# Half-width products, masks and updates in a blocked triangular inversion, with the factor's identity columns written by GpSimd

## The chip, the core and the metric

The kernel runs on one core of one Trainium2 chip. The core has five engines that work in parallel, each through its own list of instructions in order: PE (TensorE, matrix products; its weight loads are listed apart as PEld and overlap the products), DVE (VectorE), ACT (ScalarE), POOL (GpSimd) and SP, which here only issues DMAs. The metric is the device time of the run in microseconds (us); lower is better. Times of single instructions and of waits come from one execution recorded by the hardware profiler.

## What is computed

The reference is one inference step of a two-layer decoder: layer 0 mixes tokens with a gated delta rule in chunks, layer 1 with a short gated convolution; each layer also attends to 256 memory tokens, and there are 2048 prompt tokens and 64 sample tokens. The part that the change touches is the triangular solve of the delta rule in layer 0:

```
A = jnp.tril(jnp.einsum('bnhid,bnhjd->bnhij', kb, k) * decay, -1)
wu = lax.linalg.triangular_solve(A + jnp.eye(C, dtype=A.dtype), rhs, left_side=True,
                                 lower=True, unit_diagonal=True)
```

The kernel builds the inverse of I + A for 128 tokens at a time (for the 64 sample tokens in blocks of 8) and applies it as a product.

## The kernel before

**Stages.** Layer 0 takes six heads over four prompt tiles of 512 tokens and one sample tile of 64. For each head and tile it projects keys, queries, values and a gate out of 1024 inputs (`proj`: 24 products of 128x512 into one PSUM bank, named `psp` in the rows), convolves and activates them on ACT and DVE, builds the matrix and its inverse (the `wy_` jobs), scans the four chunks one after the other with the head's state (`scan`, bank `psA`) and writes the gated output. Then come the attention, the output projection, and layer 1, which has no inversion.

**Order.** Nothing is scheduled on the chip. The kernel writes its program through `Flow`, a planner: every step is a Python generator (a job), and whenever the planner's own PE clock is free, it runs the job of the highest priority that is ready by then. Ready times come from a table of costs: `mm` charges a product 3 + columns / 2.4 ns (at least 64 columns), `Eng` charges the other engines by elements, `HOPS` the way from engine to engine. Buffers are handed out by credits (`Credit`, `Sub`): a job that wants a buffer yields until one has been put back. Since each engine works in program order, an instruction whose input is late holds up everything behind it on its engine. A changed cost therefore moves instructions of unrelated jobs.

**The inversion** is `wy_inv`. One job holds a pair of chunks (`hc` = 2, both of 128 tokens; the sample tile has one of 64). It is started twice for each prompt tile, 48 times in all, with 6 levels each (`lv` = 7), and 6 times for the sample tiles, with 2 levels: 48 x 6 + 6 x 2 = 300 levels. The tile `ul` holds the inverse so far, as U (transposed) and L, each with two 128x128 matrices in 16-bit floats. `A16` (`A` in the rows, since numbers are cut from names; the listings of order print `A_1568` and the like) holds the scaled matrix. At level `li` the blocks of size 2^li on the diagonal are already inverted, and pairs of them are joined:

- PE: `pq` = A16 times L, 2 products of 128 columns. Release: the ACT copy of the level before.
- DVE: `qq` = `pq` times a mask `masks[:, li]`, 256 elements per partition, out of PSUM. The mask keeps the block below the diagonal and the diagonal itself, so that `qq` is an identity plus the blocks.
- PE: `pu`, 4 products of 128 columns: `qq` with U, and U with `qq`.
- ACT: copies `pu` back over U and L, 512 elements per partition in one instruction.

After the last level come a correction (`pe`, `ee`) and the last product into `u`. POOL works beside this: it adds the scaled identity (`M`), makes the first U, the low part `Ml` of the matrix, the tables `gm` of the decays, the low halves of the projection weights (`whl`) and of the normed input (`ht`), and small powers (`rk`, `rq`, `hr`).

The buffers `qq`, `A16`, `Ml`, `ee` and `gm` come from one ring of 12 (`NKQ`, credit `kqc`); before the change a `qq` was taken only after `pq`, and put back right behind the `pu` products.

Of the kernel before, what the change touches and what calls it, by code (L numbers as in the profile page):

```python
# [15 lines left out]
AF = mybir.ActivationFunctionType  # L16
ALU = mybir.AluOpType
# [269 lines left out]
def hybrid_kernel(  # L287
# [18 lines left out]
    fl = Flow()  # L306
# [43 lines left out]
    def wait(*flags):  # L350
        for f in flags:
            if not f.on or f.t + HOP > fl.cur.t:
                yield f
# [20 lines left out]
    kqc = Credit(fl, NKQ)  # L374
# [3 lines left out]
    def const(shape, dt, name):  # L378
        return cp.tile(shape, dt, tag=name, name=name)
# [7 lines left out]
    def psum(tag, shape, bufs, name):  # L387
        t = pp.tile(shape, F32, tag=tag, name=name, bufs=bufs)
        psum_names.add(t.tensor.name)
        return t  # L390
# [4 lines left out]
    def gbank(name):  # L395
        return psum("bank", [P, 4, P], 8, name)
# [10 lines left out]
    def k1(name, dt=F32):  # L407
        return gp.tile([P, 2, P], dt, tag="k1", name=name, bufs=NK1)
# [4 lines left out]
    def kq16(name):  # L413
        return gp.tile([P, 2, P], F16, tag="kq", name=name, bufs=NKQ)
# [439 lines left out]
    identh = const([P, P], F16, "identh")  # L854
# [5 lines left out]
    masks = const([P, 7, P], F16, "masks")  # L860
# [539 lines left out]
    def rows(x, n, C):  # L1400
        return x[:n, :n].rearrange("p (o f) -> p o f", o=1).to_broadcast([n, C, n])
# [150 lines left out]
    def wy_inv(it, i):  # L1552

        n, hc = it.n, it.hc
        lv = 7 if n == P else 3
        yield from wait(it.M_ok[i])
        M = it.M[i]  # L1560
        G.tensor_tensor(M[:n, :hc, :n], M[:n, :hc, :n], rows(identKh, n, hc), op=ALU.add)
        yield
        yield from ulc.get()
        yield from kqc.get(2)
        A16 = kq16("A16")
        V.tensor_copy(A16[:n, :hc, :n], M[:n, :hc, :n])
        UL = gp.tile([P, 4, P], F16, tag="k1", name="ul", bufs=NK1)
        U, L = UL[:n, 0:2], UL[:n, 2:4]
        yield
        yield from gc_.get()  # L1570
        pq = gbank("pq")
        for z in range(hc):
            mm(pq[:n, z, :n], A16[:n, z, :n], identh[:n, :n])
        t = fl.cur.t
        G.tensor_tensor(U[:, :hc, :n], A16[:n, :hc, :n], rows(mask_u, n, hc), op=ALU.mult)
        fl.cur.t, fl.cur.eng = t, "PE"
        yield
        V.tensor_tensor(L[:, :hc, :n], pq[:n, :hc, :n], rows(masks[:, 0], n, hc), op=ALU.mult)
        gc_.put()
        yield  # L1580
        Ml = None
        for li in range(1, lv):
            yield from gc_.get()
            pq = gbank("pq")
            for z in range(hc):
                mm(pq[:n, z, :n], A16[:n, z, :n], L[:, z, :n])
            if Ml is None:
                t = fl.cur.t
                Ml = kq16("Ml")
                G.tensor_tensor(Ml[:n, :hc, :n], M[:n, :hc, :n], A16[:n, :hc, :n], op=ALU.subtract)  # L1590
                fl.cur.t, fl.cur.eng = t, "PE"
                Mc.put()
            yield
            yield from kqc.get()
            qq = kq16("qq")
            V.tensor_tensor(qq[:n, :hc, :n], pq[:n, :hc, :n], rows(masks[:, li], n, hc), op=ALU.mult)
            gc_.put()
            yield
            yield from gc_.get()
            pu = gbank("pu")  # L1600
            for z in range(hc):
                mm(pu[:n, z, :n], qq[:n, z, :n], U[:, z, :n])
            for z in range(hc):
                mm(pu[:n, 2 + z, :n], U[:, z, :n], qq[:n, z, :n])
            kqc.put()
            yield
            if hc == 2:
                A.activation(UL[:n, :, :n], pu[:n, :, :n], AF.Copy)
            else:
                A.activation(UL[:n, 0:4:2, :n], pu[:n, 0:4:2, :n], AF.Copy)  # L1610
            gc_.put()
            yield
        yield from gc_.get()
        pe = gbank("pe")
        for z in range(hc):
            mm(pe[:n, z, :n], A16[:n, z, :n], L[:, z, :n], start=True, stop=False)
            mm(pe[:n, z, :n], Ml[:n, z, :n], L[:, z, :n], start=False, stop=True)
        yield
        kqc.put(2)
        yield from kqc.get()  # L1620
        ee = kq16("ee")
        V.tensor_tensor(ee[:n, :hc, :n], rows(identKh, n, hc), pe[:n, :hc, :n], op=ALU.subtract)
        gc_.put()
        yield
        yield from uc.get()
        yield from gc_.get()
        pu = gbank("pu1")
        for z in range(hc):
            mm(pu[:n, z, :n], ee[:n, z, :n], U[:, z, :n])
        kqc.put()  # L1630
        yield
        it.u[i] = k1("u1")
        V.scalar_tensor_tensor(it.u[i][:n, :hc, :n], pu[:n, :hc, :n], 1.0 / MS, U[:, :hc, :n], op0=ALU.mult, op1=ALU.add)
        gc_.put()
        ulc.put()
        fl.set(it.u_ok[i])
# [170 lines left out]
    def head_tile(hd, t):  # L1807
# [13 lines left out]
        for i, (blk, w, dst) in enumerate(((6 + h, wk, kt_), (h, wq, qt_), (12 + h, wv, v_))):  # L1821
# [23 lines left out]
            if i == 0:  # L1845
                fl.spawn(3, chain(start, wy_decay(it)), "decay")
                fl.spawn(3, chain(start, wy_k(it, dn[0])), "wy_k")
                for z in range(it.nh):
                    fl.spawn(1, wy_inv(it, z), f"inv{z}")
            elif i == 1:  # L1850
                fl.spawn(3, chain(start, wy_q(it, dn[1])), "wy_q")
            else:
                fl.spawn(3, chain(start, wy_v(it, dn[2])), "wy_v")
# [449 lines left out]
```

## Time and profile before

| | |
|---|---|
| time, median of 3 runs | 2224.36 us (2221.85 to 2230.78) |
| time of the profiled execution | 2225.13 us |
| its span, first to last instruction | 2223.4 us |
| PE busy | 2147.2 us, 97% |
| DVE, ACT, POOL busy | 1488.9, 1120.7, 714.3 us |
| instructions of PE, DVE, ACT, POOL | 16176, 4228, 2952, 901 |
| levels of the inversion, and the stretch they lie in | 300, from 128 to 1050 us |

A row of busy time gives the union of an engine's instructions. PE's products are pipelined: one lasts some 0.2 to 0.4 us in the record, but the next one starts much sooner, so the distance between starts is what a product costs when PE has enough to do.

### The profile page before, as it was taken

The numbers are of one execution on the slowest core, as the hardware profiler recorded it, in microseconds if no ns is written. First come the engines' busy times: TensorE is split into PE (matmuls) and PEld (weight loads), VectorE is DVE, ScalarE is ACT, GpSimd is POOL, SyncE is SP. The second block draws the span as 40 slices with busy tenths as digits, with TensorE's granted clock in tenths as the row PEclk, the third lists the DMA queues.
The fourth block names the chain that finished last, engine by engine and source line by source line (L and its number), as shares of the span: only waits on it lengthen the run. The fifth ranks groups of instructions, "written<-read, shape, count | busy, mean of one in ns | idle before, by whom it ended". The sixth has DMA issues, their size and how long they took to land.

```text
span 2223.4 us, 43011 instructions
## 1 busy us (share of the span) xinstructions
PE 2147.2 (97%) x16176; PEld 1298.0 (58%) x16176; DVE 1488.9 (67%) x4228; ACT 1120.7 (50%) x2952; POOL 714.3 (32%) x901
## 2 busy tenths in 40 slices
PE   6889989999999999999999999999999999999998
PEld 5467657667666666666555454455444456555457
DVE  6988887887889878777777566355342437675354
ACT  5757665566657656566566345134221226653221
POOL 5655334442434433433222335012110212201322
PEclk9989999999999999999999999999999999999999
DMA  4201020201122102002134443022010111223433
GB/s 134 64 13 37 16 49 9 55 30 27 39 70 41 50 6 46 31 6 69 56 102 143 142 152 114 15 68 80 31 54 10 53 49 58 69 72 129 129 112 118
DMA packets 113634, 141.50 MB, mean 64 GB/s; under 512 B 50193, under 2 KB 67857, under 8 KB 113425
## 3 DMA queue, kind: packets, MB, share of 16 engines
q1 hardware_dynamic: 113424, 138.75, 20.5%
q8 instruction: 127, 2.08, 0.4%
q14 instruction: 83, 0.67, 0.1%
HBM read 99.22 MB, written 39.49 MB: 62 GB/s over the span
## 4 chain that ended last, share of the span: by engine, by line
PE 58%; DVE 3%; ACT 1%; issue 1%; DMA 1%; POOL 0%; POOLq 0%; DVEq 0%; ACTq 0%
PE psp L330 49%; PE psA L330 2%; PE psc L334 1%; PE pu L330 1%; PE po L330 1%; PE psc L330 1%; PE rb L330 1%; DVE wmx L281 1%; PE pq L330 1%; PE pqk L330 0%; DVE amx L281 0%; PE pkk L330 0%; DMA wraw<-in_wo 0%; DVE apT L281 0%; PE po L334 0%
## 5 line engine op out<-in xcount | busy, mean ns | idle before, releaser
L330 PE MATMUL psp<-ht,whl 128*128 128x512 f16 x5376 | 1270.0, 380 | 0.0
L330 PEld LDWEIGHTS <-whl 128*128 128x128 f16 x9408 | 753.6, 98 | 650.1 <-issue 12.6
L281 POOL TENSOR_TENSOR whl<-wraw,whl 128x512 f16<-128x512 f32 x184 | 216.8, 1182 | 448.0 <-ACT whl L281 400.2
L330 PE MATMUL psp<-hl,whl 128*128 128x512 f16 (+1 forms) x1728 | 342.4, 357 | 0.0
L281 ACT ACTIVATE ul<-pu 128x512 f16<-128x512 f32 x300 | 168.3, 582 | 79.6 <-PE pu L330 76.8
L281 ACT ACTIVATE wraw<-wraw,wsc 128x512 f32<-128x512 f32 (+1 forms) x186 | 131.7, 712 | 76.3 <-DVE wsc L281 44.6
L281 DVE SCALAR_TENSOR_TENSOR cacc<-psp,cws,cacc 128x511 f32<-128x511 f32 (+2 forms) x216 | 159.4, 738 | 10.1 <-ACT cacc L281 9.8
L281 POOL TENSOR_TENSOR nsq<-nsq 128x512 f32<-128x512 f32 (+2 forms) x105 | 100.6, 960 | 194.3 <-ACT nsq L281 149.1
L281 DVE TENSOR_TENSOR qq<-pq,masks 128x256 f16<-128x256 f32 x300 | 118.0, 407 | 51.1 <-PE pq L330 49.2
L281 DVE TENSOR_REDUCE wmx<-wraw 128x1 f32<-128x1024 f32 (+1 forms) x93 | 111.5, 1201 | 31.6 <-DMA wraw<-in_wb 24.5
L281 ACT ACTIVATE wg<-psp,hisc 128x512 f32<-128x512 f32 x64 | 44.0, 687 | 171.6 <-PE psp L330 171.4
L281 ACT ACTIVATE nsq<-xo 128x512 f32<-128x512 f32 (+1 forms) x72 | 41.4, 580 | 150.8 <-DVE xo L281 86.8
L281 ACT ACTIVATE whl<-wraw 128x512 f16<-128x512 f32 x184 | 114.8, 626 | 2.7
L281 DVE SCALAR_TENSOR_TENSOR xo<-psp,isc,xo 128x512 f32<-128x512 f32 (+1 forms) x72 | 49.6, 688 | 95.2 <-PE psp L330 95.2
L281 DVE SCALAR_TENSOR_TENSOR wg<-wg,psp 128x512 f32<-128x512 f32 x64 | 43.6, 681 | 87.8 <-ACT wg L281 87.8
L330 PEld LDWEIGHTS <-A 128*128 128x128 f16 x792 | 69.4, 100 | 41.1 <-issue 10.4
L281 ACT ACTIVATE ape<-psc,amx,sa 128x256 f32<-128x256 f32 x128 | 70.8, 561 | 31.7 <-DVE amx L281 31.6
L330 PE MATMUL pu<-ul,qq 128*128 128x128 f16 (+1 forms) x588 | 81.8, 224 | 3.9 <-DVE qq L281 3.1
L330 PE MATMUL pq<-ul,A 128*128 128x128 f16 (+1 forms) x588 | 77.0, 224 | 4.6 <-ACT ul L281 2.6
L330 PE MATMUL pu<-qq,ul 128*128 128x128 f16 (+1 forms) x588 | 81.2, 223 | 0.0
L281 POOL TENSOR_TENSOR rk<-sse,mhalf 128x4 f32<-128x4 f32 (+1 forms) x30 | 27.6, 919 | 159.9 <-DVE sse L281 118.8
L281 DVE SCALAR_TENSOR_TENSOR raw<-psp,wisc,cg 128x512 f32<-128x512 f32 x24 | 18.0, 749 | 86.9 <-PE psp L330 86.8
(344 smaller groups left out, 3641.0 us busy)
## 6 DMA issues: line engine op xcount, KB each, us to landing
br_sp<-wg SPq DMA_DIRECT2D x64, 256.0 KB, 2.0
brl<-br_sp SPq DMA_DIRECT2D x64, 256.0 KB, 2.9
wraw<-in_wb SPq DMA_DIRECT2D x28, 512.0 KB, 3.5
wraw<-in_wa SPq DMA_DIRECT2D x24, 512.0 KB, 3.5
xk<-in_x SPq DMA_DIRECT2D x64, 128.0 KB, 2.9
wraw<-in_wo SPq DMA_DIRECT2D x16, 512.0 KB, 3.4
xo<-in_x SPq DMA_DIRECT2D x32, 256.0 KB, 3.5
x_sp<-xo SPq DMA_DIRECT2D x32, 256.0 KB, 2.4
```

Source lines behind the costliest of these rows:

```text
L281: return f(out, *args, **kw)
L330: nc.tensor.matmul(out, lhsT=lhsT, rhs=rhs, start=start, stop=stop)
L334: nc.tensor.transpose(out, in_, ident)
```

## The change

At a level, only half the columns change: of L, in each pair of blocks the first block's columns; of U, the second's. The other columns of the products repeat what is there already, and the second blocks' columns of `qq` are plain identity columns. The change uses this in all 300 levels:

- `pq` and `pu` are made for 64 columns instead of 128 (32 instead of 64 in the sample tiles). The moving operand is read in runs of 2^li elements with gaps as long; the result lies packed in PSUM. The stationary operands keep their size.
- The DVE mask works on half the elements, with the mask and the output read and written in those runs.
- The ACT copy becomes two, one for U and one for L, of 128 elements each, written in runs.
- The identity columns of `qq` are now written by POOL (`unit`, 300 new instructions: identity times identity into the other half). The first is placed ahead of the levels, each further one right behind the `pu` products of the level before. Its buffer is thus taken a level ahead, directly after the former `qq` was put back.

```
-                mm(pq[:n, z, :n], A16[:n, z, :n], L[:, z, :n])
+                mm(pq[:n, z, :nb], A16[:n, z, :n], first[0][:, z])
...
-            V.tensor_tensor(qq[:n, :hc, :n], pq[:n, :hc, :n], rows(masks[:, li], n, hc), op=ALU.mult)
+            mask = halves(masks[:n, li:li + 1], li)[0].to_broadcast([n, hc, nb, 1 << li])
+            V.tensor_tensor(qf[:, :hc], pq[:n, :hc, :nb], mask, op=ALU.mult)
...
-                mm(pu[:n, z, :n], qq[:n, z, :n], U[:, z, :n])
+                mm(pu[:n, z, :nb], qq[:n, z, :n], second[1][:, z])
...
-                mm(pu[:n, 2 + z, :n], U[:, z, :n], qq[:n, z, :n])
+                mm(pu[:n, 2 + z, :nb], U[:, z, :n], qf[:, z])
+            t = fl.cur.t
             kqc.put()
+            if li + 1 < lv:
+                yield from kqc.get()
+                qq = unit(li + 1)
+            fl.cur.t, fl.cur.eng = t, "PE"
...
-                A.activation(UL[:n, :, :n], pu[:n, :, :n], AF.Copy)
+            A.activation(second[1][:, :hc], pu[:n, :hc, :nb], AF.Copy)
+            A.activation(first[0][:, :hc], pu[:n, 2:2 + hc, :nb], AF.Copy)
```

The new functions are

```
+        def halves(x, li):
+            v = x[:, :, :n].rearrange("p z (b h s) -> p z b h s", h=2, s=1 << li)
+            return v[:, :, :, 0], v[:, :, :, 1]
+        def unit(li):
+            qq = kq16("qq")
+            i2 = halves(idh, li)[1].to_broadcast([n, hc, n >> (li + 1), 1 << li])
+            G.tensor_tensor(halves(qq[:n], li)[1][:, :hc], i2, i2, op=ALU.mult)
+            return qq
```

Since the planner's costs of these steps change, all engines' lists are rearranged from the first inversion on. On PE the first `pu` products of the program stood like this (names: `ht` is the normed input, `whl` a projection's weights; in brackets the engines whose semaphores the instruction waits for):

```order
L330 MATMUL psp<-ht,whl 128x512
L330 LDWEIGHTS qq [waits PE_49,DVE_49]
L330 MATMUL pu<-ul,qq 128x128 [waits Pool_49]
L330 LDWEIGHTS qq
L330 MATMUL pu<-ul,qq 128x128
L330 LDWEIGHTS ul
L330 MATMUL pu<-qq,ul 128x128
```

and in the changed kernel the first ones read

```order
L330 MATMUL psp<-ht,whl 128x512
L330 LDWEIGHTS qq [waits DVE_49,Pool_49]
L330 MATMUL pu<-ul,qq 128x64 [waits PE_49]
L330 LDWEIGHTS qq
L330 MATMUL pu<-ul,qq 128x64
L330 LDWEIGHTS ul
L330 MATMUL pu<-qq,ul 128x64
```

The products have half the columns, as many weight loads stand before them, and the load of `qq` now waits for POOL as well as for DVE.

On POOL, the difference around the first two inversions is this (`A_1568` and `A_1606` are their matrices; `+` is new, the bare rows stand in both):

```order
 L281 TENSOR_TENSOR ul<-A_1606,mask_u 128x256
 L281 TENSOR_TENSOR ht<-nhs,ht 128x256
+L281 TENSOR_TENSOR qq<-identh 128x64x2
 L281 TENSOR_TENSOR Ml<-M,A_1568 128x256
 L281 TENSOR_TENSOR gm<-sLh,ghl 128x256 x2
+L281 TENSOR_TENSOR qq<-identh 128x64x2
+L281 TENSOR_TENSOR Ml<-M,A_1606 128x256
+L281 TENSOR_TENSOR ht<-nhs,ht 128x256 x3
+L281 TENSOR_TENSOR qq<-identh 128x32x4 x2
+L281 TENSOR_TENSOR rk<-sse,mhalf 128x4
+L281 TENSOR_TENSOR gm<-sLh,ghl 128x256 x2
+L281 TENSOR_TENSOR qq<-identh 128x16x8 x2
```

The identity columns of a level (`128x64x2`: 64 runs of 2, for both chunks) stand between the work for the next tiles, sometimes behind a power (`rk`) that waits for DVE.

On ACT, at the same place:

```order
-L281 ACTIVATE kd<-pk,eGlG 128x128 x4
-L281 ACTIVATE kt<-cacc 128x512
-L281 ACTIVATE cacc<-psp,cws 128x512
-L281 ACTIVATE ul<-pu 128x512 x2
+L281 ACTIVATE kt<-cacc 128x512
+L281 ACTIVATE cacc<-psp,cws 128x512
+L281 ACTIVATE kd<-pk,eGlG 128x128 x4
+L281 ACTIVATE ul<-pu 128x64x2 x4
+L281 ACTIVATE dd<-pd 128x256
 L281 ACTIVATE ht<-nhs 128x256
 L281 ACTIVATE qt<-cacc 128x512
```

Two copies of 512 elements have become four of 128 (64 runs of 2), and the neighbouring steps of the key's chain have changed places.

## Rows read from the trace of the kernel before

**Rows 1.** The page: busy time and share of each engine; granted PE clock, tenths, 40 slices.

```profile
PE 2147.2 (97%) x16176; PEld 1298.0 (58%) x16176; DVE 1488.9 (67%) x4228; ACT 1120.7 (50%) x2952; POOL 714.3 (32%) x901
...
PEclk9989999999999999999999999999999999999999
```

**Rows 2.** The page: the chain that ended last, shares by engine.

```profile
PE 58%; DVE 3%; ACT 1%; issue 1%; DMA 1%; POOL 0%; POOLq 0%; DVEq 0%; ACTq 0%
```

**Rows 3.** Stretches: us, busy PE, PEld, DVE, ACT, POOL (instructions), PE clock, DMA share, GB/s.

```profile
0.00:125.00 125.00, 97.01 (x616) 62.98 (x617) 96.74 (x279) 76.49 (x206) 74.00 (x111) 0.97 0.28 88
125.00:1055.00 930.00, 902.49 (x7488) 620.19 (x7487) 758.08 (x2443) 587.57 (x1792) 370.59 (x512) 0.99 0.14 35
1055.00:2223.40 1168.40, 1147.68 (x8076) 614.82 (x8075) 634.05 (x1508) 456.60 (x954) 269.74 (x279) 0.99 0.26 84
```

**Rows 4.** Who PE waited for from 125 to 1055 us: total, times, longest.

```profile
PE psA L330 <- ACT vh L281: 4.3, 1, 4.3
PE pu L330 <- DVE qq L281: 3.1, 6, 1.2
PE pq L330 <- ACT ul L281: 2.6, 5, 1.6
```

**Rows 5.** Groups of the inversion's steps, 125 to 1055 us: busy, mean ns | idle before.

```profile
L330 PE MATMUL pq<-ul,A 128*128 128x128 f16 x576 | 74.5, 224 | 4.6 <-ACT ul L281 2.6 <-DVE ssq L281 1.2 <-issue 0.4
L330 PE MATMUL pu<-ul,qq 128*128 128x128 f16 x576 | 79.2, 224 | 3.9 <-DVE qq L281 3.1
L281 DVE TENSOR_TENSOR qq<-pq,masks 128x256 f16<-128x256 f32 x288 | 115.7, 415 | 48.1 <-PE pq L330 46.4 <-PE psp L330 0.4
L281 ACT ACTIVATE ul<-pu 128x512 f16<-128x512 f32 x288 | 165.6, 595 | 76.5 <-PE pu L330 73.7 <-PE psp L330 1.6
```

**Rows 6.** PE in order of time: start, us, instruction, count; products of 128 and 64 columns.

```profile
536.79 0.28 PE L330 MATMUL pu<-ul,qq 128*128 128x128 f16 x2
...
537.12 0.28 PE L330 MATMUL pu<-qq,ul 128*128 128x128 f16 x2
537.23 0.81 PE L330 MATMUL psp<-ht,whl 128*128 128x512 f16 x3
...
539.23 0.60 PE L330 MATMUL psp<-hs_t,whl 128*128 128x64 f16 x15
539.66 0.47 PE L330 MATMUL psA<-vh,kd 128*128 128x128 f32 x2
```

**Rows 7.** Groups nearest to the new steps, 125 to 1055 us.

```profile
L281 DVE TENSOR_TENSOR o<-qs,psA 128x128 f32<-128x128 f32 x89 | 24.7, 278 | 0.0
L281 ACT ACTIVATE jk<-pqt 128x128 f32<-128x128 f32 x88 | 24.5, 278 | 9.1 <-PE pqt L334 6.9
L281 POOL TENSOR_TENSOR hm<-nhs,hm 128x128 f16<-128x128 f32 x8 | 3.4, 430 | 8.2 <-ACT hm L281 7.1 <-DVE qq L281 1.2
L281 POOL TENSOR_TENSOR gm<-sLh,ghl 64x64 f16<-64x64 f16 x12 | 3.2, 290 | 0.0
L281 POOL TENSOR_TENSOR ul<-A,mask_u 128x256 f16<-128x256 f16 x46 | 31.1, 686 | 21.7 <-DVE A L281 20.4 <-POOL dd L281 0.8 <-PE pq L330 0.2
L281 POOL TENSOR_TENSOR rk<-sse,mhalf 128x4 f32<-128x4 f32 x23 | 23.3, 1011 | 126.9 <-DVE sse L281 99.6 <-DVE halo L281 12.8 <-ACT kd L281 8.1
```

**Rows 8.** ACT in order of time: four copies with a pointer scale; two of 512 elements.

```profile
523.09 1.17 ACT L281 ACTIVATE kd<-pk,eGlG 128x128 f32<-128x128 f32 x4
...
537.27 1.08 ACT L281 ACTIVATE ul<-pu 128x512 f16<-128x512 f32 x2 [0.59 <-PE pu L330]
```

**Rows 9.** POOL and DVE at 200 us; one DVE step: group; durations min/median/max.

```profile
200.00 2.09 POOL L281 TENSOR_TENSOR ht<-nhs,ht 128x256 f16<-128x256 f32 x3 [4.53 <-ACT ht L281]
...
200.88 0.59 DVE L281 SCALAR_TENSOR_TENSOR cacc<-halo,cws,cacc 128x1 f32<-128x1 f32 x1
...
L281 DVE SCALAR_TENSOR_TENSOR cacc<-halo,cws,cacc 128x3 f32<-128x3 f32 x160 | 48.9, 305 | 0.0
...
L281 DVE SCALAR_TENSOR_TENSOR cacc<-halo,cws,cacc x162: 198/209/3218, 119.5 to 1009.9; 128x1 f32<-128x1 f32 x54, 128x2 f32<-128x2 f32 x54, 128x3 f32<-128x3 f32 x54
```

More of the change, by code (lines that the diff above doesn't have):

```diff
@@ L1581, in wy_inv @@
         Ml = None
+        def halves(x, li):
+            v = x[:, :, :n].rearrange("p z (b h s) -> p z b h s", h=2, s=1 << li)
+            return v[:, :, :, 0], v[:, :, :, 1]
+        idh = identh[:n, :n].rearrange("p (o f) -> p o f", o=1)
+        def unit(li):
[4 more added lines that the diff above has]
+        yield from kqc.get()
+        qq = unit(1)
+        fl.cur.t, fl.cur.eng = t, "PE"
         for li in range(1, lv):
+            nb = n >> (li + 1)
+            first, second = halves(L, li), halves(U, li)
+            qf = halves(qq[:n], li)[0]
             yield from gc_.get()
-            pq = gbank("pq")
+            pq = gbank("pq").rearrange("p c (b s) -> p c b s", s=1 << li)
             for z in range(hc):
-                mm(pq[:n, z, :n], A16[:n, z, :n], L[:, z, :n])
+                mm(pq[:n, z, :nb], A16[:n, z, :n], first[0][:, z])
+            t = fl.cur.t
             if Ml is None:
-                t = fl.cur.t
                 Ml = kq16("Ml")
                 G.tensor_tensor(Ml[:n, :hc, :n], M[:n, :hc, :n], A16[:n, :hc, :n], op=ALU.subtract)
-                fl.cur.t, fl.cur.eng = t, "PE"
                 Mc.put()
+            fl.cur.t, fl.cur.eng = t, "PE"
             yield
-            yield from kqc.get()
-            qq = kq16("qq")
-            V.tensor_tensor(qq[:n, :hc, :n], pq[:n, :hc, :n], rows(masks[:, li], n, hc), op=ALU.mult)
+            mask = halves(masks[:n, li:li + 1], li)[0].to_broadcast([n, hc, nb, 1 << li])
+            V.tensor_tensor(qf[:, :hc], pq[:n, :hc, :nb], mask, op=ALU.mult)
             gc_.put()
@@ L1599, in wy_inv @@
             yield from gc_.get()
-            pu = gbank("pu")
+            pu = gbank("pu").rearrange("p c (b s) -> p c b s", s=1 << li)
             for z in range(hc):
-                mm(pu[:n, z, :n], qq[:n, z, :n], U[:, z, :n])
+                mm(pu[:n, z, :nb], qq[:n, z, :n], second[1][:, z])
             for z in range(hc):
-                mm(pu[:n, 2 + z, :n], U[:, z, :n], qq[:n, z, :n])
+                mm(pu[:n, 2 + z, :nb], U[:, z, :n], qf[:, z])
+            t = fl.cur.t
             kqc.put()
+            if li + 1 < lv:
+                yield from kqc.get()
+                qq = unit(li + 1)
+            fl.cur.t, fl.cur.eng = t, "PE"
             yield
-            if hc == 2:
-                A.activation(UL[:n, :, :n], pu[:n, :, :n], AF.Copy)
-            else:
-                A.activation(UL[:n, 0:4:2, :n], pu[:n, 0:4:2, :n], AF.Copy)
+            A.activation(second[1][:, :hc], pu[:n, :hc, :nb], AF.Copy)
+            A.activation(first[0][:, :hc], pu[:n, 2:2 + hc, :nb], AF.Copy)
             gc_.put()
```

## The prediction

> **What bounds the kernel now.** I read the page first, then the stretches, then who waits for whom on PE. PE is busy 97% of the span at nearly its full granted clock [rows 1], and 58% of the chain that ended last is PE's, against 3% for DVE and 1% for ACT [rows 2]. The change lives in the stretch from 125 to 1055 us: there PE is busy for 902.5 of 930 us at a granted clock of 0.99 (the 2.4 GHz level but for a short time), DVE for 758.1 (82%), ACT for 587.6 (63%) and POOL for 370.6 (40%) [rows 3]. PE hardly ever stands still for the inversion: its products waited 3.1 us in all for the mask and 2.6 us for the copy back [rows 4], and no row of that list names POOL as the one waited for, though PE already uses tables, the first U and `Ml` that POOL makes. The other way round, DVE stood 46.4 us and ACT 73.7 us until the inversion's products came [rows 5]. So the inversion is not a chain of latencies that sets the end; it is work that lies between the projections' products. What counts is how much PE time it takes. A step saved on DVE or ACT is worth little, a PE time saved is worth nearly itself.
>
> **The terms.** The sum is made against the profiled execution, 2225.1 us; the median of the runs is 2224.4, so 0.7 us lie between.
>
> PE. Per level of two chunks there are 2 products `pq` and 4 `pu`; the rows count 576 for `pq` and 576 for one of the two kinds of `pu` [rows 5], the other kind has as many: 1728 products of 128 columns. In an undisturbed place 8 of them, each with its own weight load, take from 536.79 to 537.23 us: 55 ns each. Fifteen products of 64 columns, also each with its own weight load, take from 539.23 to 539.66 us: 28.7 ns each [rows 6]. So halving the columns gives 26.3 ns x 1728 = 45.5 us. The 36 small products of the sample tiles I take at nothing: even if each fell by as much, it would be 0.9 us.
>
> The bounds of that term: the moving operand is now read in runs of 2 to 64 elements with gaps, for which no row exists. If such a read cost twice a plain one, a product would stay at 55 ns and the term would be 0; if only the two shortest runs (2 and 4 elements, 2 of 6 levels) cost that, it would be 30 us. I take the full 45.5, since the rows with 64 columns are the nearest.
>
> A rule speaks against this term. The rows show 55 ns for 128 columns and 28.7 ns for 64, a weight load before each. The Trainium skill (TensorE: Matmul & The Clock Gate, "Back-to-back issue gap") says that in a stream of weight load and product both set the spacing, and gives about 81 ns for 128 columns; its section on LDWEIGHTS has that load grow with the stationary columns, which stay 128 here. By that rule halving the moving columns would save next to nothing. The trace does not agree with the number, and its 64-column row has the same loads; I keep the rows' price and carry the rule's outcome as a rival.
>
> DVE. The mask goes from 256 to 128 elements: 415 ns before; the nearest row, a product of two tiles of 128 elements out of PSUM, has 278 [rows 5, 7]. That is 137 ns x 288 = 39.5 us less on an engine that is 82% busy. It lies beside PE's work: nothing.
>
> ACT. One copy of 512 elements becomes two of 128. Two of 512 take 1.08 us [rows 8], the last of them 0.6 us [rows 5], so 0.48 us lie between starts. Four copies of 128 elements with a scale from memory take 1.17 us, at most 0.29 each [rows 8]; a quarter of the 512-element spacing, 0.12, is the other end. A pair thus takes 0.24 to 0.58 us of the engine in place of 0.48: between 69 us less and 29 us more over 288 levels. At the upper end ACT is at some 617 of 885 us, 70%. As a delay, a pair ends 0.12 to 0.29 us plus a duration of 0.28 [rows 7] behind its start, against 0.6: no longer than before. Cover: the projections' products. Cost nothing.
>
> POOL. 300 new instructions, 288 of them of 128 elements. The nearest row, two inputs and 128 elements, has 430 ns; the ends are 290 (64 elements on 64 partitions) and 686 (256 elements) [rows 7]. That is 84 to 198 us, and I take 124: POOL goes from 371 to some 495 us in a stretch of 885, 56%. What hides it: the instruction is put in behind `pu` of one level and needed at `pu` of the next, and between these lie a pair of copies, `pq` and a mask, at least 0.4 + 0.28 us, and whatever projection products PE has in between. A POOL step of 0.43 us fits; what does not fit is a queue in front of it. Behind it wait on POOL's list `Ml`, `gm`, the powers and the low halves `whl` and `ht`; `rk` had idle time on POOL before it already [126.9 us in 23 cases, rows 7], so a delay of some tenths there meets no one.
>
> The ring. A `qq` is now held from one level into the next; it is put back and taken again at the same point, so an inversion in flight holds 3 of 12 buffers all the time, and four of them would leave none for `gm`. I cost this at nothing as long as two or three are in flight.
>
> Sum: 2225.1 - 45.5 = 2179.6, say 2180. What is late next when PE is lighter: DVE, at 758 - 39.5, some 719 of 885 us, 81%. It doesn't become the bound.
>
> **The rivals.**
>
> *Half of it is lost to standing time.* With 45 us less PE work in 930, there is less to put between the steps of a level, and DVE is held up more. The trace shows how: at 200.88 us a DVE step over a single element took 0.59 us while POOL was at work, and ended at 201.47, about when the second of POOL's three steps did (200.00 + 2/3 x 2.09 = 201.4); the group's median is 209 ns, its mean 305, its longest 3218 [rows 9]. That is 160 x 96 ns = 15 us at 371 us of POOL; with 495 us it would be some 20. The Trainium skill (GPSIMD Engine Reference, "Specifications") has the two engines share their SBUF interfaces, with contention where a DVE instruction has two SBUF inputs, which this agrees with. PE was not busy for 27.5 us of the stretch [rows 3]; if that doubles, 2180 + 27 = 2207. For it: every engine's list is new. Against it: the masks themselves read PSUM and get shorter.
>
> *A product of 64 columns in runs, or behind its weight load, costs what one of 128 does.* Then the change gives PE nothing and only the shorter mask remains: 2225, within the 0.5%. Against it stand rows 6.
>
> *Slower: POOL comes late, and PE stands.* The load of `qq` waits for POOL, and everything on PE stands behind it. POOL's list holds three powers per prompt tile, 72 in all, of 1 us each, that wait for DVE; before `rk` POOL stood 5.5 us on average [rows 7]. A `qq` put behind such a power is late by as much as the power. If each of the 72 held PE for 1 us, that is 72 us: 2180 + 72 = 2252. It decides from 57 / 72, 0.8 us for each, on. Against it: POOL makes inputs of PE through the same list now, and no wait of PE on POOL shows.
>
> *More than the columns.* The mask is 0.14 us shorter, the copy up to 0.2, in each level; PE's waits for them (5.7 us, rows 4) and part of the other standing time go too, 10 to 20 us: 2160 to 2170.
>
> **How the numbers follow.** The forecast (2170 to 2195) has 0.60; half lost (2195 to 2213) 0.18; no cheaper product 0.10; slower 0.05; more than the columns 0.07. 0.5% of 2224 is 11 us, about what a measurement of this kernel can tell from no change: faster means below 2213, and the forecast, the half-lost case and the greater gain lie there, 0.85 together; the unchanged product gives 0.10 for the same, late POOL 0.05 for slower. For 8 in 10 I take the forecast, the half-lost case and the greater gain from 2160 on: 2160 to 2213 leaves out the unchanged product and the late POOL, 0.15, and the little below 2160.
>
> **What the changed profile would show.** The `pq` and `pu` products stand 28 to 30 ns apart in undisturbed rows, at the levels with runs of 2 as at those with 64; 55 there would make the second rival right. The stretch of the inversions gets some 45 us shorter and the one after it keeps its length. The mask takes some 280 ns, a copy 250 to 290, `qq` on POOL some 430; POOL is at about 500 us in the stretch. In the list of PE's waits no row with `qq` from POOL has more than a few us; many short ones would make the third rival right. PE's share of the stretch stays at 96 to 97%; 94% with waits spread over DVE steps would be the first. A wait of `gm` for its buffer, with PE standing at `pd`, would show the ring as the limit that I put at nothing.

## The result, and the profile after

| | before | changed |
|---|---|---|
| time, median (range, runs) | 2223.88 us (2221.85 to 2230.78, 4) | 2197.97 us (2195.57 to 2206.61, 4) |
| profiled execution, its span | 2225.13, 2223.4 us | 2195.57, 2193.9 us |
| ratio to before | | 0.9885, 95% interval 0.985 to 0.9921 |

The change saves 26 us in the medians and 29.6 us between the two profiled executions. Forecast were 45 us (2180). The median of 2198 lies in the range that was given 8 in 10 (2160 to 2213), but 3 us outside the forecast's own 2170 to 2195, in the interval of the rival in which half is lost to standing time.

The page of the changed kernel, first its busy times and PE's granted clock in tenths (against [rows 1]), then the shares of the chain of waits that ended last (against [rows 2]):

```profile
PE 2107.4 (96%) x16176; PEld 1258.5 (57%) x16176; DVE 1461.5 (67%) x4228; ACT 1080.9 (49%) x3252; POOL 831.2 (38%) x1201
...
PEclk9989999999999999999999999999999999999999
...
PE 52%; DVE 2%; issue 0%; ACT 0%; POOL 0%; DMA 0%; POOLq 0%; DVEq 0%; ACTq 0%
```

The stretches of the changed kernel, with the columns of [rows 3]: us, busy PE, PEld, DVE, ACT and POOL, granted clock, DMA share, GB/s.

```profile
125.00:1025.00 900.00, 861.13 (x7495) 580.06 (x7494) 729.77 (x2437) 546.28 (x2088) 486.14 (x811) 0.98 0.14 37
1025.00:2193.90 1168.90, 1148.61 (x8068) 614.84 (x8064) 634.18 (x1511) 457.59 (x956) 270.28 (x279) 0.99 0.26 83
```

The stretch behind the inversions is as long as it was (1168.9 against 1168.4 us; from the product on behind which PE's two lists are the same, 1017.2 against 1017.3 us are left), so everything happened in the stretch of the inversions, 900 us in place of 930. There PE is busy for 41.4 us less (902.5 to 861.1), and stands for 11.4 us more (27.5 to 38.9); its share of the stretch is 95.7%.

The groups of the inversion's steps from 125 to 1025 us (busy, mean ns of one | idle before), against [rows 5]:

```profile
L330 PE MATMUL pu<-ul,qq 128*128 128x64 f16 x576 | 58.7, 196 | 10.1 <-DVE qq L281 4.4 <-POOL qq L281 3.2 <-POOL M L281 1.9
L330 PE MATMUL pu<-qq,ul 128*128 128x64 f16 x576 | 58.6, 196 | 0.0
L330 PE MATMUL pq<-ul,A 128*128 128x64 f16 x576 | 56.7, 196 | 7.0 <-ACT ul L281 6.5
...
L281 ACT ACTIVATE ul<-pu 128x128 f16<-128x128 f32 x576 | 120.2, 283 | 67.5 <-PE pu L330 60.6 <-PE pq L330 4.7 <-PE psp L330 1.4
L281 POOL TENSOR_TENSOR qq<-identh 128x128 f16<-128x128 f16 x287 | 115.0, 419 | 22.1 <-PE pu L330 7.7 <-PE pd L330 6.2 <-PE pe L330 2.2
L281 DVE TENSOR_TENSOR qq<-pq,masks 128x128 f16<-128x128 f32 x288 | 75.8, 283 | 35.3 <-PE pq L330 34.6
```

The mask takes 283 ns (415 before), one copy 283 (595 for the one of 512), the identity columns 419. PE's waits for these steps have grown from 3.1 to 4.4 us (mask) and from 2.6 to 6.5 us (copy), and there is a new one, `qq` from POOL, 3.2 us.

PE in order of time, in a place without waits (start, us, instruction, count), to set beside [rows 6]:

```profile
538.57 0.22 PE L330 MATMUL pu<-ul,qq 128*128 128x64 f16 x2
538.63 0.22 PE L330 MATMUL pu<-qq,ul 128*128 128x64 f16 x2
538.69 0.22 PE L330 MATMUL pu<-ul,qq 128*128 128x64 f16 x2
538.75 0.22 PE L330 MATMUL pu<-qq,ul 128*128 128x64 f16 x2
```

Two products every 0.06 us: 30 ns for 64 columns, each with its own weight load, against 55 ns before. In the whole trace the median distance between two such products is 31 ns with runs of 2 and of 4 elements and 29 ns with runs of 8 to 64. So the columns came off PE as forecast. The question of the experiments is where 16 to 20 of 45 us went behind that.

### The profile page after: what moved, and what is told of

It reads as the page before. It is cut to its first block, busy times and chain, and to the rows that moved or that the text cites. A ratio compares the mean times of both kernels' runs of the same rounds, so it can differ in the third digit from the quotient of the medians.

```text
span 2193.9 us, 44074 instructions
## 1 busy us (share of the span) xinstructions
PE 2107.4 (96%) x16176; PEld 1258.5 (57%) x16176; DVE 1461.5 (67%) x4228; ACT 1080.9 (49%) x3252; POOL 831.2 (38%) x1201
## 4 chain that ended last, share of the span: by engine, by line
PE 52%; DVE 2%; issue 0%; ACT 0%; POOL 0%; DMA 0%; POOLq 0%; DVEq 0%; ACTq 0%
PE psp L330 46%; PE psc L334 1%; PE po L330 1%; PE psc L330 1%; PE rb L330 1%; PE po L334 0%; PE psA L330 0%; DVE amx L281 0%; PE pam L330 0%; PE psT L330 0%; PE spo L330 0%; DVE nhs L281 0%; DVE cacc L281 0%; POOL nsq L281 0%; DVE apT L281 0%
## 5 line engine op out<-in xcount | busy, mean ns | idle before, releaser
L330 PEld LDWEIGHTS <-whl 128*128 128x128 f16 x9408 | 747.8, 98 | 654.6 <-issue 11.2
L281 ACT ACTIVATE ul<-pu 128x128 f16<-128x128 f32 x600 | 123.4, 279 | 70.1 <-PE pu L330 63.2
L281 POOL TENSOR_TENSOR qq<-identh 128x128 f16<-128x128 f16 x300 | 118.2, 412 | 22.1 <-PE pu L330 7.7
L281 ACT ACTIVATE nsq<-xo 128x512 f32<-128x512 f32 (+1 forms) x72 | 41.4, 582 | 148.7 <-DVE xo L281 87.3
L281 DVE SCALAR_TENSOR_TENSOR xo<-psp,isc,xo 128x512 f32<-128x512 f32 (+1 forms) x72 | 49.6, 689 | 97.1 <-PE psp L330 97.1
L281 DVE TENSOR_TENSOR qq<-pq,masks 128x128 f16<-128x128 f32 x300 | 77.9, 278 | 35.5 <-PE pq L330 34.7
L330 PEld LDWEIGHTS <-A 128*128 128x128 f16 (+1 forms) x792 | 65.4, 101 | 42.3 <-issue 14.2
L330 PE MATMUL pu<-ul,qq 128*128 128x64 f16 x588 | 61.0, 196 | 10.7 <-DVE qq L281 4.4
L281 POOL TENSOR_TENSOR ht<-nhs,ht 128x256 f16<-128x256 f32 (+1 forms) x64 | 54.7, 871 | 33.8 <-ACT ht L281 33.5
```

The costliest lines, as they stand in the source:

```text
L281: return f(out, *args, **kw)
```

## Experiments: POOL or the order

Three theories were stated. **P**: POOL's identity columns cost it, through DVE or as late `qq`. **O**: the rearranged lists are worse than those of before. **C**: with thinner cover (less of PE's own work between the steps of a level) more of the standing time shows, in any order. Four kernels cross POOL's work with the order.

**The changed order without POOL's columns.** POOL's step is planned but not issued, and with the masks cut to their diagonal the inverse is left out. The four tiles that are set once take their room from the ring of buffers, which has 9 here in place of 12.

```
-            G.tensor_tensor(halves(qq[:n], li)[1][:, :hc], i2, i2, op=ALU.mult)
+            qq = qst[qs]
+            o = halves(qq[:n], li)[1][:, :hc]
+            fl.op("POOL", 150.0 + 1.66 * count(o), o, [identh])
...
-            V.scalar_tensor_tensor(masks[:, li], mk_d, 1.0 / MS, sLh, op0=ALU.mult, op1=ALU.mult)
+            V.scalar_tensor_tensor(masks[:, li], mk_d, 0.0, sLh, op0=ALU.mult, op1=ALU.mult)
```

> The changed kernel in its own order, but the 300 identity columns aren't written at all: the products read tiles set once at the start, and the masks keep only their diagonal so that numbers stay finite (the inverse is left out thereby; the instructions on PE, DVE and ACT are the same). The planner is still charged for them, so PE's list stands as in the changed kernel. Of the 45.5 us that PE's columns give, some 16 to 20 went missing. Theory P (the columns on POOL cost it: PE waits for them, and POOL holds up DVE): about 2182 us. Theory O (the new lists stand worse than the old ones for the same work): about 2197. Theory C (with less PE work between the steps of a level, whatever the order, more standing time shows): about 2197.

Measured: 2198.38 us (2191.32 to 2201.55), ratio 0.9877 [0.9853, 0.9902]: no faster than the changed kernel.

**All of the change in the order of before.** The planner is charged the old costs, so that PE's list is word for word that of before, with 64 columns in place of 128, and DVE's stands in the same order too.

```
-                mm(pq[:n, z, :nb], A16[:n, z, :n], first[0][:, z])
+                mm(pq[:n, z, :nb], A16[:n, z, :n], first[0][:, z], wide=2)
...
-            A.activation(second[1][:, :hc], pu[:n, :hc, :nb], AF.Copy)
-            A.activation(first[0][:, :hc], pu[:n, 2:2 + hc, :nb], AF.Copy)
+            fl.op("ACT", 52.0 + 0.83 * 2 * hc * n, UL, [pu])
+            nc.scalar.activation(second[1][:, :hc], pu[:n, :hc, :nb], AF.Copy)
+            nc.scalar.activation(first[0][:, :hc], pu[:n, 2:2 + hc, :nb], AF.Copy)
```

> All steps of the change, identity columns on POOL too, but the planner is charged with the costs of the full-width steps and with nothing for the identity columns: PE's list stands word for word as before the change. Theory P: 2197 or a little more, since POOL's work is the same and the planner doesn't know of it. Theory O: about 2180. Theory C: about 2197.

Measured: 2192.38 us (2189.69 to 2198.98), ratio 0.9863 [0.9836, 0.9891].

**The order of before, and no POOL columns.** The edits of both.

> Half-width products, masks and copies in the order of before, without the identity columns (left out as in the run without POOL in the new order, masks with their diagonal alone). Theory P: 2180. Theory O: 2180. Theory C: about 2197.

Measured: 2192.39 us (2187.67 to 2193.88), ratio 0.9851 [0.9831, 0.9871].

**The kernel before, with POOL's 300 steps written into a tile that nobody reads.**

```
+            dm = gp.tile([P, 2, P], F16, tag="dm", name="dm", bufs=1)
...
+            nc.gpsimd.tensor_tensor(halves(dm[:n], li)[1][:, :hc], i2, i2, op=ALU.mult)
```

> The kernel before in its own order, with 300 identity-column writes added on POOL into a tile that nobody reads, at the places where the change has them. It prices POOL's work by itself (its place in POOL's queue and what it holds up on DVE), without PE waiting for it. Theory P: 10 to 15 us slower than before, about 2236. Theories O and C: within 4 us of before, 2224.

Measured: 2225.57 us, before 2225.61 beside it, ratio 1.0 [0.9987, 1.0012]. The stretch from 125 to 1055 us of this run, and POOL's new group in it:

```profile
125.00:1055.00 930.00, 901.57 (x7488) 617.45 (x7486) 765.66 (x2442) 588.40 (x1792) 487.69 (x812) 0.99 0.14 35
...
L1592 POOL TENSOR_TENSOR dm<-identh 128x128 f16<-128x128 f16 x287 | 121.8, 425 | 10.0
```

POOL has 117 us more (370.6 before), DVE is busy for 7.6 us more (758.1 before, [rows 3]), and the end does not move. P's 10 to 16 us fall: beside PE's full-width work POOL's steps cost nothing by themselves, and without them neither order is faster in the medians. With four executions a kernel, a few microseconds in the light kernels are not excluded: in the old order PE still waits 3.9 us for `qq` from POOL.

**Which copy first.** The next `pq` needs only L, and PE's waits of 6.5 us for the copy were the largest. A fourth theory, **D**, has the new steps themselves at fault, the pair of copies among them. Two kernels swap the two copies, one in each order:

```
-            A.activation(second[1][:, :hc], pu[:n, :hc, :nb], AF.Copy)
             A.activation(first[0][:, :hc], pu[:n, 2:2 + hc, :nb], AF.Copy)
+            A.activation(second[1][:, :hc], pu[:n, :hc, :nb], AF.Copy)
```

> The changed kernel with the two copies of a level in the other order: L first, then U. The next pq needs only L; every engine's list is otherwise the same, word for word. Theory D (the new steps themselves make the missing microseconds, and among them the pair, whose second half is the one that pq waits for): PE's row pq waiting for the copy falls from 6.5 us to about 3, and the time falls by 3 to 6 us, to 2192 to 2195. Theory C (the thinner cover shows more of every wait of the chain, whichever step it is): the 0.16 us between the two starts comes off one wait and in part goes back on to pu, which needs U: 0 to 3 us less, 2195 to 2198.

> All of the change in the order of the kernel before (run e2_old_order), with the copy of L ahead of that of U; lists the same but for this. Theory D: 3 to 6 us less than e2's 2192.4, 2186 to 2189. Theory C: 2189 to 2192. If this is below both kernels it is the version to keep.

Measured: in the changed order 2203.53 us (2200.06 to 2211.14), ratio 0.9913 [0.9893, 0.9933]; in the old order 2190.95 us (2189.18 to 2191.92), ratio 0.9849 [0.983, 0.9868]. D falls: the swap gains nothing in the one order (the median is some 5 us higher, but the interval overlaps with that of the changed kernel, so that no loss is shown) and 1.4 us in the other, within the noise. But the pair is a third comparison of the orders: new against old it is 2198.0 to 2192.4, 2198.4 to 2192.4 and 2203.5 to 2191.0, some 6 us twice, with intervals that overlap, and 12.6 once, where they do not. Taken together, the 14 executions of the new order have a median of 2200.6 us (2191.3 to 2211.1), the 12 of the old one 2191.2 (2187.7 to 2199.0).

**A place of it.** PE's busy time and count, granted clock, DMA share and GB/s from 245 to 255 us and in the 70 us behind, in the changed kernel, then in the run with all of the change in the old order:

```profile
245.00:255.00 10.00, 6.00 (x58) 0.71 0.00 0
255.00:325.00 70.00, 66.83 (x648) 0.99 0.19 37
...
245.00:255.00 10.00, 9.72 (x74) 1.00 0.00 1
255.00:325.00 70.00, 63.67 (x562) 1.00 0.17 40
```

The two other kernels of the new order have 5.52 and 5.58 us busy from 245 to 255 us, at 0.85 and 0.86, whether POOL writes its columns or not; the others of the old order 9.79 and 9.71, at 1.00. PE in the changed kernel at this place (in brackets the idle time before and who ended it), and DVE beside it:

```profile
245.65 1.06 PE L330 MATMUL pqk<-qt,kt 128*128 128x128 f32 x8
248.76 0.49 PE L330 MATMUL psA<-S,kt 128*128 128x128 f32 x2 [2.05 <-DVE S L281]
...
252.62 0.79 PE L330 MATMUL psA<-R,u 128*128 128x128 f32 x2 [1.87 <-DVE qs L281]
```

```profile
245.86 1.26 DVE L281 SCALAR_TENSOR_TENSOR nhs<-xk,gain,rb 128x256 f32<-128x256 f32 x3
247.03 0.41 DVE L281 SCALAR_TENSOR_TENSOR u<-pu,ul 128x256 f32<-128x256 f32 x1
247.37 0.73 DVE L281 SCALAR_TENSOR_TENSOR cacc<-psp,cws,cacc 128x509 f32<-128x509 f32 x1
248.02 0.42 DVE L281 SCALAR_TENSOR_TENSOR cacc<-halo,cws,cacc 128x3 f32<-128x3 f32 x1
248.37 0.33 DVE L281 SCALAR_TENSOR_TENSOR S<-S,eGl,psA 128x128 f32<-128x128 f32 x1
```

The scan's step `S` stands in DVE's list behind `nhs`, `u` and `cacc` of other jobs, with DVE busy without a gap, and the next thing in PE's list is the scan's product that needs `S`. PE stands for 3.9 us in these two waits, and the granted clock falls to the lower of its two levels within the same ten microseconds (0.71 on the mean). Only the new order loses here. But the place shows how the order costs, not how much: in the 70 us behind it is the old order that stands more (6.3 against 3.2 us; 6.7 and 4.7 in its two others, against 2.2 and 1.7). From 125 to 325 us PE is busy for only 1.3 us less in the changed kernel than in the old order. From 325 to 700 us there are 2.6 us more (363.7 against 366.3 busy) and from 700 to 1000 us another 1.6 (289.3 against 290.9). The loss is spread over the whole stretch: some 5.5 us of standing in these two profiled executions, about the difference in time.

## Experiments: what a column is worth

The old order leaves 33 of 45.5 us. Is the rest C?

**A longer chain, in the kernel before and in the light one.** One idle copy of 128 elements more on ACT per level, ahead of the copy back:

```
+            dm = gp.tile([P, 2, P // 2], F16, tag="dm", name="dm", bufs=1)
+            nc.scalar.activation(dm[:n, :hc, :n // 2], pu[:n, :hc, :n // 2], AF.Copy)
```

> The kernel before with one idle copy more per level on ACT (half of pu, 128 elements, into a tile that nobody reads) ahead of the copy back; PE's list unchanged. Each level's chain gets 0.16 to 0.3 us longer (128-element copies of the changed kernel start 158 ns apart and last 278), 300 levels, 47 to 84 us of ACT in all. If the chain lies wholly under PE's work: 2224, no change. Theory C: the cover of the kernel before hides most of it: 0 to 4 us more, 2224 to 2228. Rival S (a longer chain costs the same in either kernel): the same loss as in e8.

> The changed kernel in the old order (e2_old_order, 2192.4) with the same idle copy of 128 elements ahead of the pair in each level; PE's list is that of e7 but for the halved columns. Theory C: with 45 us less of PE's work between the steps, the same lengthening shows more: at least twice the loss of e7, and 4 to 12 us over e2, 2196 to 2204. Rival S: the same loss as e7, within 2 us.

Measured: 2236.9 us (2224.75 to 2240.88), ratio 1.005 [1.0033, 1.0067], so 12.7 us more than before, by the interval 7 to 15 (one of its nine executions, 2224.75 us, was no longer than the kernel before); and 2195.6 us (2193.64 to 2199.81), ratio 0.9875 [0.9857, 0.9893], 3.2 us more than the same kernel without it, where the intervals overlap. C wanted the light kernel to lose at least twice as much; it lost less. C in this form falls, and the difference between the two stays unexplained. What it does show stands in the profile of the first of them: PE's wait for the copy from 125 to 1067 us, and the new step.

```profile
PE pq L330 <- ACT ul L281: 8.7, 11, 3.3
...
L1608 ACT ACTIVATE dm<-pu 128x128 f16<-128x128 f32 x288 | 80.9, 281 | 67.2 <-PE pu L330 64.0 <-remote 2.4
```

The wait grows from 2.6 us [rows 4] to 8.7. So the chain of a level was not wholly covered by PE's other work, even before the change.

**One part alone, in the old order.** Only `pu` and its copies, then only `pq`, its mask and POOL's columns. Of the first, the edit of the products:

```
-                mm(pu[:n, z, :n], qq[:n, z, :n], U[:, z, :n])
+                mm(pu[:n, z, :nb], qq[:n, z, :n], second[1][:, z], wide=2)
...
-                mm(pu[:n, 2 + z, :n], U[:, z, :n], qq[:n, z, :n])
+                mm(pu[:n, 2 + z, :nb], U[:, z, :n], qf[:, z], wide=2)
```

> One part alone, in the order of the kernel before (PE's list word for word): only the four products pu have half the columns and the copy back is the pair; pq, the mask of 256 elements and the whole of qq are as before, nothing is new on POOL. 1152 products of 1728: 26.3 ns x 1152 = 30.3 us of PE's columns. All of the change in this order gave 33 of 45.5 us, 0.73. Theory C (where PE has other work to do a column counts in full, where it stands for the chain of latencies it counts nothing; the same mixture for either kind of product): 0.73 x 30.3 = 22 us less, 2199 to 2206. Theory L (a level's chain counts as run e7 had it, some 12 us for 0.16 us in each level, and the pair ends 0.16 us before the copy of 512): 12 us more, 2187 to 2194.

> The other part alone, in the same order: pq and the mask in half the columns, the identity columns by POOL; pu and the copy of 512 elements are as before. 576 products: 15.1 us of columns. Theory C: 0.73 x 15.1 = 11 us less, 2210 to 2217, and this and the run with pu alone add up to the 33 us of the whole. Theory L: the mask is 0.14 us shorter in each level, some 10 us more, 2200 to 2207; the two parts then add up to more than the whole.

Measured: `pu` alone 2203.93 us (2202.53 to 2206.41), 20.5 us of 30.3; `pq` alone 2209.78 us (2207.81 to 2212.09), 14.7 of 15.1; before beside them 2224.46. By the intervals `pu` brings 16 to 23 us, `pq` 11 to 17 and the whole 24 to 36. Together 35.2, the whole 33: within these the parts add up. `pu` alone is where C has it, `pq` alone between C and L.

**The mirror.** In the kernel before, an idle product of 64 columns ahead of each real one, into the place that this overwrites (here at `pq`; the same stands ahead of the four `pu`):

```
+                nc.tensor.matmul(pq[:n, z, :n // 2], lhsT=A16[:n, z, :n], rhs=L[:, z, :n // 2], start=True, stop=True)
                 mm(pq[:n, z, :n], A16[:n, z, :n], L[:, z, :n])
```

> The mirror of the change: in the kernel before, each of the 1728 products pq and pu has an idle product of 64 columns more ahead of it, with the same stationary operand and into the place that the real product then overwrites; all lists are otherwise as before. PE gets 28.7 ns x 1728 = 49.6 us more. If a fixed share of the inversion lies where PE stands anyway (three quarters of each column count, whichever way): 0.73 x 49.6 = 36 us more, 2255 to 2264. Theory C (the cover: the more work PE has, the less it stands, so added columns cost nearly themselves, and removed ones bring back less and less; pq alone brought 14.7 of 15.1, pu alone 20.5 of 30.3): 45 to 50 us more, 2269 to 2275.

Measured: 2257.52 us (2254.38 to 2259.53), ratio 1.0146 [1.0129, 1.0163], so 32.7 us (by the interval 29 to 36) for 49.6 us of columns. That is 0.66 of them, where the removal in the same order brought 0.73 (by its interval 0.53 to 0.80). C's 45 to 50 us fall; a fixed share is nearer to what was measured. The 0.97 of `pq` alone doesn't fit it, unless its shorter mask has a part in it, as L has it.

**Where the share arises.** PE's order is the same in all these kernels, so the same product can be looked up in each. The rows give the first and last start (us) of two groups: `pkk<-kqs`, whose first stands at the first sample tile, and `pe<-ul,A`, whose last closes the inversions. Before, then all of the change in the old order, then the mirror:

```profile
L330 PE MATMUL pkk<-kqs x12: 222/246/270, 318.2 to 1037.2; 128*64 128x64 f32 x12
L330 PE MATMUL pe<-ul,A x102: 213/219/289, 158.1 to 1053.4; 128*128 128x128 f16 x96, 64*64 64x64 f16 x6
```

```profile
L330 PE MATMUL pkk<-kqs x12: 222/246/270, 309.8 to 1004.5; 128*64 128x64 f32 x12
L330 PE MATMUL pe<-ul,A x102: 213/219/314, 155.3 to 1020.8; 128*128 128x128 f16 x96, 64*64 64x64 f16 x6
```

```profile
L330 PE MATMUL pkk<-kqs x12: 222/246/270, 315.4 to 1067.2; 128*64 128x64 f32 x12
L330 PE MATMUL pe<-ul,A x102: 213/219/230, 156.4 to 1083.7; 128*128 128x128 f16 x96, 64*64 64x64 f16 x6
```

And the count of one of the three kinds of product up to the first mark (125 to 318.2 us, before):

```profile
L330 PE MATMUL pu<-ul,qq 128*128 128x128 f16 x130 | 19.6, 241 | 2.8 <-DVE qq L281 2.4
```

So 390 of the 1728 products stand ahead of the first mark and 1338 between the marks. By 26.3 ns removed or 28.7 ns added:

| kernel | columns ahead of the mark, us | mark moved, us | columns between the marks, us | stretch between (735.2 before), us |
|---|---|---|---|---|
| all, old order | -10.3 | -8.4 | -35.2 | 711.0 (-24.2) |
| `pu` alone | -6.8 | -8.1 | -23.5 | 721.6 (-13.6) |
| `pq` alone | -3.4 | -6.4 | -11.7 | 726.3 (-8.9) |
| mirror | +11.2 | -2.8 | +38.4 | 768.3 (+33.1) |

Between the marks the time follows the columns, at 0.58 to 0.76 of them when removed and 0.86 when added. Ahead of the mark it does not: 11.2 us more columns made the mark no later, and 3.4 us less brought nearly twice that. So what is missing lies at different places. Of all the change in the old order, 11.0 of 35.2 us go missing between the marks and only 1.9 of 10.3 ahead of the first. Of the mirror 14.0 us go missing ahead of it, where 11.2 us were added and the mark moved forward by 2.8, and 5.3 of 38.4 behind it. These are single executions, and the runs of before spread from 2216 to 2232 us in all; but the run with POOL's 300 unread steps, whose list on PE is the same as that of before, has the first mark at 318.0 us and 735.5 us between the marks.

PE's busy time between the marks, of before, of all of the change in the old order and of the mirror:

```profile
318.20:1053.40 735.20, 722.01 (x5948) 1.00 0.15 37
...
309.80:1020.80 711.00, 691.27 (x5950) 1.00 0.16 39
...
315.40:1083.70 768.30, 758.67 (x7324) 1.00 0.14 36
```

PE stands for 13.2 us there in the kernel before, for 19.7 with the columns removed and for 9.6 with columns added. That is C's direction: 6.5 of the 11.0 us that go missing are new standing time. In the other 4.5 us PE shows as busy, although the columns are gone and the clock is as high. What fell with the mirror is C's size, not this mechanism. Not all of the new standing time need be lost cover: with `pu` alone, where nothing is new on POOL, PE stands for 18.1 us between the marks, but in the old order without POOL's columns only for 15.8, with 705.4 us between the marks. That is one execution, and the median of that run is no shorter.

Ahead of the first mark, 14.3 us of standing lie in the first 200 us of before (185.68 busy in its row below), more than between the marks, in a stretch not a third as long. So PE isn't the only limit there. One of these waits, 4.3 us of `psA` for `vh` [rows 4], 3.2 us in the run with POOL's unread steps, isn't among those of the mirror.

**The granted clock.** It works in the same direction. The stretches from 125 to 325 us, of before and of the mirror:

```profile
125.00:325.00 200.00, 185.68 (x1575) 131.26 (x1574) 163.87 (x551) 129.97 (x407) 87.80 (x127) 0.94 0.11 28
```

```profile
125.00:325.00 200.00, 191.66 (x1998) 139.71 (x1995) 166.01 (x556) 133.83 (x414) 89.57 (x130) 0.98 0.11 28
```

With more to do PE was granted 0.98 in place of 0.94, and stood for 8.3 in place of 14.3 us. Over the whole span the clock was 0.989 in the profiled execution of before, 0.986 in the changed kernel's and 0.993 in the mirror's. Since the clock has two levels, 1.2 and 2.4 GHz, twice the missing part is time at the lower one: some 49, 61 and 32 us. If PE were at work in all of it, 12 us more cost 6 us in the changed kernel, and 17 us less give back 8 in the mirror: at most a third to a half of what is missing from either sum (16 and 17 us).

The executions on record say how closely the two go together. Over 43 of the kernel before, 0.001 less of the mean granted clock goes with 1.3 us more (correlation -0.78); within the 14 kernels, 110 executions in all, with 1.4 us. At that rate the three comparisons of the orders, 6, 6 and 13 us in the means, come to 3, 3 and 7 us at an equal clock, and the shares of removed and added columns to 0.76 and 0.74. So about half of the order's price goes with a lower clock. Whether the clock makes the time longer, or the same waits do both, is not shown by this.

**Is it the half clock itself?** One more run fills PE's waits between 138 and 175 us with 194 idle products, in the best kernel so far:

```
+        k = FILL.get(seen[0], 0)
+        seen[0] += 1
+        for _ in range(2 * k):
...
+            nc.tensor.matmul(o, lhsT=identh, rhs=r, start=True, stop=True)
...
+        idle(out)
         nc.tensor.matmul(out, lhsT=lhsT, rhs=rhs, start=start, stop=stop)
```

> Run e6_old_order_l_first with 194 idle products of 64 columns (identity times identity, 5.3 us of PE) in ten places between 138 and 175 us of the span, each ahead of a product that waits there anyway and into its own place in PSUM, which it then overwrites. Nothing else changes. Theory K (the stretches at half clock between 140 and 175 us, 20 to 31 us in the changed kernel against 20 before, come from PE standing there, and they cost): the granted clock stays at 1.0 there, and the time falls by 3 to 8 us, to 2183 to 2188. If the half clock is only a sign of the same waits and costs nothing by itself, the time stays at 2190 to 2193; if the idle products are in the way, it is above 2193.

Measured: 2192.35 us (2191.29 to 2196.83), against 2190.95 without; ratio 0.986 [0.9847, 0.9874]. PE's busy time and granted clock in four stretches, without the idle products, then with them:

```profile
135.00:145.00 10.00, 7.90 (x89) 0.83 0.01 2
145.00:155.00 10.00, 7.95 (x109) 0.83 0.10 30
155.00:165.00 10.00, 7.89 (x65) 0.66 0.13 39
165.00:175.00 10.00, 8.82 (x92) 0.66 0.14 42
```

```profile
135.00:145.00 10.00, 7.14 (x154) 1.00 0.01 2
145.00:155.00 10.00, 9.52 (x192) 1.00 0.11 31
155.00:165.00 10.00, 7.50 (x81) 0.73 0.13 39
165.00:175.00 10.00, 9.20 (x118) 0.76 0.15 42
```

The clock rose, to 1.00 in the first two stretches and to 0.73 and 0.76 in the others, where K had 1.0 throughout, and K's 3 to 8 us did not come. So at this place a higher clock was not worth more than the idle products took. Whether PE was not what the end waited for, or the 5.3 us of idle products took back what the clock gave, this run doesn't tell apart. No run tried the clock at another place.

## Why the prediction was right, and where it was off

- **The columns.** Right: 30 ns in place of 55, in runs with gaps. The rival of the product that gets no cheaper is out, and so, for this stream, is the rule it rested on: the Trainium skill (TensorE: Matmul & The Clock Gate, "Back-to-back issue gap") gives about 81 ns for a stream of weight loads and products of 128 columns, and this trace has 55 for those and 30 for 64 behind the same load.
- **"A PE time saved is worth nearly itself."** This is the step that failed. The sum took 45.5 us at 1.0; in an unchanged order they are worth 33, 0.73 (0.53 to 0.80). The prediction's support was that PE stood for only 27.5 us of the stretch [rows 3] and named few waits [rows 4]. But as the columns went, PE stood more: between the marks its standing time went from 13.2 to 19.7 us in the same order (18.1 with `pu` alone), and to 9.6 where columns were added. So part of what was taken off PE had filled waits. That PE shows as busy in waits that are too short to be seen, since a record of a product lasts 0.2 to 0.4 us, several times the distance to the next, would fit the 4.5 us behind that; it is argued, not shown.
- **"Every engine's list is new"** stood in the text with no price. It cost some 6 us, in one pair 12.6. At 245 to 255 us it can be seen how: a step that PE needs stands in DVE's list behind work of other jobs. The prediction asked of DVE what its busy time sums up to (81%, which came), not what stands ahead of what in its list.
- **The half-lost rival** had the interval (2195 to 2213) and half of the mechanism: less to put between the steps of a level. Its size was off: it had the 27.5 us of standing double, and they became 38.9. The other half was wrong. DVE is held by POOL, as the Trainium skill has it (GPSIMD Engine Reference, "Specifications": interfaces to SBUF shared with VectorE, contention where its instruction has two SBUF inputs); from 125 us to the last product `pe<-ul,A` DVE is busy for 765 us in the run with 300 unread steps, and for 756 to 759 in the kernel before, the one with a longer chain and the mirror, which have the same list on DVE. But the end stayed at 2225.6.
- **POOL late** did not come: 3.2 us of waits for `qq` (3.9 in the old order), and about the same time without the step. The ring, put at nothing, names no wait.
- **DVE and ACT off the path** was half right. The mask fell by 132 ns, and a pair of copies of 283 ns each, whose starts lie 157 ns apart, ends no later than one of 595, with no loss that any run shows. But 0.16 us added to each level's copy in the kernel before cost 12.7 us, so such a step does lie on the path in part, and the 14.7 of 15.1 us of `pq` alone may contain something of its shorter mask. No run separates that.
- **The later stages** kept their length, as forecast.

That the range held the result is thus in part luck: it took in a rival whose time came, by a mechanism that is half of the rival's and a price of the order that nobody had put down. Of the 45.5 us some 12 are lost in any order and some 6 to the new one; both come from medians whose intervals reach 6 to 8 us to either side. What stays open is what the rest of the 12 is beside the 6.5 us of standing time, whether POOL's `qq` has a part in these, what the clock adds to either loss, and why the longer chain cost more in the heavier kernel.

The best kernel is the change in the order of before with L copied first: 2190.95 us, 0.9849 [0.983, 0.9868]. From the same without the swap (2192.38) no measurement here tells it apart.

## What to carry to other kernels

A busy share of 97% does not price a saved microsecond at one microsecond: work taken off the busiest engine may have filled waits, and here PE's standing time rose as the work fell. When a planner rearranges the lists, run the change once in the old order, so that its own worth and that of the new order are told apart; here they were 33 and -6 us. Adding the same work in idle form gave about the share that removing it brought, 0.66 and 0.73 per microsecond. But the two shares arose at different places, so the agreement in this one case is no rule.

## What was not expected of the hardware

- Products whose moving operand is read in runs of 2 to 64 elements with gaps start 29 to 31 ns apart with 64 columns (medians by length of run), nearly as the plain ones do (28.7 ns, [rows 6]).
- 117 us more of POOL's work that nobody waits for, beside DVE at 82%, cost 0.0% [-0.13%, +0.12%].
- The mean granted clock of an execution went with the time of the same program: 0.993 in the fastest run of the kernel before (2216.1 us), 0.987 in the slowest (2232.1); and it was higher with more work on PE (0.992 to 0.994 in the mirror's four executions) and lower in the changed kernel (0.982 to 0.987 in its four), though with the same products in the old order and L copied first it is 0.986 to 0.990, not clearly below before's 0.987 to 0.993.
